# One decoder layer on one core: the down projection in seven products of block pairs, with sums of halves made ahead

## The chip, the cores and the metric

The kernel runs on 1 core of one Trainium2 chip. Its time is the device time of one execution in microseconds; the time of a kernel is the median of its runs. The profile is of one execution, taken by the hardware profiler. Of the engines, TensorE (PE) multiplies matrices, VectorE (DVE), ScalarE (ACT) and GpSimd (POOL) work on tiles elementwise, and SyncE (SP) issues most transfers. Each engine runs its instructions in the order in which they are written, and SP's transfers form one queue.

## The reference

A decoder layer on x of 1024 rows (T) by 1024 columns (D): two attention mixers, a SwiGLU feed-forward of width 2816 (F), layer norm after each, and scale, shift and gate from a conditioning vector c. The change is in the feed-forward:

```python
def swiglu(u, w_gate_up, w_down):
    h = jnp.einsum('btd,df->btf', u, w_gate_up)
    hg, hu = jnp.split(h, 2, axis=-1)
    return jnp.einsum('btf,fd->btd', jax.nn.silu(hg) * hu, w_down)
...
    x = layer_norm(DEEPNORM_ALPHA * x + (1.0 + gate_m) * y, ln1_g[l], ln1_b[l])
    u = x * (1.0 + scale_f) + shift_f
    y = swiglu(u, w_gate_up[l], w_down[l])
    x = layer_norm(DEEPNORM_ALPHA * x + (1.0 + gate_f) * y, ln2_g[l], ln2_b[l])
```

All of it is float32. `gate_f` is one of six vectors of 1024 that come from c through w_ada.

## The kernel before

**Numbers.** A float32 operand is split into a high part, which ScalarE rounds to fp32r, and a low part, which VectorE makes as the difference. A product of two operands is then three matmuls (high by high, high by low, low by high), each of 128x128 by 128x512 (`mac`, L191 to L193). `split` (L169, L170) does this for a whole operand; class `Pairs` does it for the weights of gate and up (L144, L145), and class `Weights` for others (L78, L79).

**Gate and up.** The loop over p (22 values, `NF`) makes 128 columns of F at a time for gate and up, all 1024 rows. Gate and up by the two halves of D, times the two halves of D by the two halves of the rows, would be eight products of halves; the kernel makes seven, some of them of sums (`product`, L1033, with its matmul L1041). A pass is one p: seven products, i = 0 to 6, of 12 matmuls each (4 blocks of D by three). POOL makes the sums of the weights for the next pass (`gu.add`, L126 to L132), SP loads those of the pass after that (`gu.load`, L112, two loads of 128x1024, 512 KB each), and a product's weights are split three products ahead (`g_prepare(n + 3)`). The bank of a product is copied by ScalarE (L1551, L1557) or added by VectorE (L1561) to what becomes the gate `g[0]` and `g[1]`, one for each half of the rows. At i = 6 VectorE multiplies gate and up (L1567, L1568), and SP stores both halves of h to scratch `h_d` (L1570).

Beside the loop run generators that move one step at a time: `last_ada` makes the gate vector `gates[5]` in steps at i = 3 and 6, with its weights in the tiles a_raw and a_lo and its sum in another; `ada_steps` does the like for other vectors earlier in the kernel, with L1009 as its matmul. Both split an accumulated sum and sum it over the partitions with a matmul by ones.

**Down projection.** h times w_down: 8 blocks of 128 rows by 2 halves of 512 columns by 22 blocks of F, three matmuls each, 1056. The weights are multiplied by `gates[5]` on POOL (L62) before they are split, so that the product can be added as it is. F is taken in groups:

```python
groups = [2, 3, 4, 3, 3, 3, 4]
```

For a group, every block of rows and every half of the columns gets a bank (`pd`), the matmuls of the group's F, and one VectorE addition into the row of z (L1627, 112 of them). While a group runs, the h of the next is loaded (`h_load`) and split (`h_prepare`), and the weights by `ws.step`. In the last group the statistics of each finished half row are taken (`half_stats`, L1272), and each row is normalized: `norm_shared` for the first seven (ScalarE, then its `finish` on VectorE and POOL, L1303 and L1304, and the store), and the shorter `norm_quick` (L1287 to L1292) for the last.

**Order.** It is written by hand (`tc.manual_schedule`): each engine runs its instructions in the program's order. A tile of a pool with n buffers waits until the n-th tile before it in that pool and tag is done with.

Of the kernel before, what the change touches and what calls it, by code (L numbers as in the profile page):

```python
# [149 lines left out]
def decoder_layer(ctx: ExitStack, tc: tile.TileContext, I, out, dbg=None):  # L150
# [83 lines left out]
    groups = [2, 3, 4, 3, 3, 3, 4]  # L234
    down_pool = lambda f: "low" if sum(f >= e for e in np.cumsum(groups)) % 2 else "bigu"
    for f in range(NF):
        for c in range(2):
            ws.add(I["w_down"][f * P:(f + 1) * P, c * 512:(c + 1) * 512], 1,
                   lambda c=c: gates[5][:, c * 512:(c + 1) * 512],
                   pair_dest(wd_t, f, lambda f: down_pool(f), "wd"))  # L240
# [744 lines left out]
    def ada_steps():  # L985
        for m in (2, 3, 4):
# [12 lines left out]
            if m == 2:  # L999
# [4 lines left out]
                yield  # L1004
                for t in range(2):
                    s = slice(t * TH, (t + 1) * TH)
                    ps = ps_2.tile([P, TH], F32, name="p2")
                    for x in range(2):
                        nc.tensor.matmul(ps, ones_r, hl[x][:, s], start=x == 0, stop=x == 1)  # L1009
# [591 lines left out]
    f0, ends, nxt = 0, [], 3  # L1601
    for gi, n in enumerate(groups):
        fs = range(f0, f0 + n)
        f0 += n
        last = gi == len(groups) - 1
        todo = [] if last else list(range(f0, f0 + groups[gi + 1]))
        prepare_at = {0: (), 3: (1, 3, 5), 4: (1, 2, 4, 6)}[len(todo)]
        for f in todo[:2]:
            if f not in h_raw:
                h_load(f)  # L1610
        for tb in range(NB):
            c = slice(tb * P, (tb + 1) * P)
            if tb in prepare_at:
                f = todo.pop(0)
                h_prepare(f)
                ws.step()
                ws.step()
                if len(todo) > 1:
                    h_load(todo[1])
            for eh in range(2):  # L1620
                es = slice(eh * 512, (eh + 1) * 512)
                pd = ps_f.tile([P, TH], F32, name="pf")
                for i, f in enumerate(fs):
                    wd, h = wd_t[f][0], hs[f]
                    mac(pd, (h[:, 0, c], h[:, 1, c]), (wd[:, 0, es], wd[:, 1, es]), i == 0, i == n - 1)
                z = zrow(tb)[:, es]
# [87 lines left out]
```

## Time and profile before

| | us |
|---|---|
| median of 3 runs (lowest, highest) | 1805.76 (1805.56, 1806.23) |
| the profiled execution | 1804.71 |
| its span (first to last instruction) | 1802.9 |
| gate and up, p = 0 to 21 | 1152.67 to 1555.60 |
| down projection, first to last matmul | 1555.60 to 1794.97 |
| after the last matmul | 7.93 |

The span is what the profile shows from the first instruction to the last; the profiled execution took 1.8 us more, and 1.05 us less than the median of the runs. The times of all views are counted from the start of the span. Each engine has a row of busy time; the row PEclk is the clock that TensorE was granted in 40 equal slices, where 9 is 90% or more. The chain of waits follows the work that ended last back from the end.

### The profile page before, as it was taken

Reading aid. Unit: us, or ns where it says so; the run is one execution under the profiler, and the core shown is the slowest. Engines: PE = TensorE matmul, PEld = TensorE weight load, DVE = VectorE, ACT = ScalarE, POOL = GpSimd, SP = SyncE. Lnnn points to the kernel's source line nnn. Section 1 sums busy time; section 2 is a strip of 40 time slices with the busy share of each in tenths; the row PEclk is TensorE's granted clock in tenths of the full one; section 3 lists DMA queues with packets and bytes.
Section 4 is the critical chain, followed back from the end, with each engine's and each line's share of the span. In section 5 each row is a group of like instructions: output and inputs, shape, how many; then the busy total and the mean of one; then the engine's idle time right before and its main releaser. Section 6 shows DMA issues by size and latency. Waiting matters only on the chain.

```text
span 1802.9 us, 24555 instructions
## 1 busy us (share of the span) xinstructions
PE 1786.3 (99%) x8906; PEld 1469.5 (82%) x8906; DVE 1147.7 (64%) x2051; ACT 810.3 (45%) x1720; POOL 619.2 (34%) x401
## 2 busy tenths in 40 slices
PE   9999999999999999999999999999999999999998
PEld 7888888888888888888788888888888888888886
DVE  7655566566656776558657865766675444764567
ACT  6544544444445677764442224734333333321122
POOL 0232233233233332125205644156663333531223
PEclk9999999999999999999999999999999999999999
DMA  9222333333332332266576333153332222442222
GB/s 363 88 71 81 97 85 92 100 87 106 90 83 83 91 94 72 79 237 234 181 231 238 144 108 109 36 166 110 110 101 86 82 82 88 163 139 72 97 73 93
DMA packets 93081, 213.83 MB, mean 119 GB/s; under 512 B 15072, under 2 KB 24864, under 8 KB 92960
## 3 DMA queue, kind: packets, MB, share of 16 engines
q1 hardware_dynamic: 92352, 210.61, 35.6%
q8 instruction: 70, 1.15, 0.3%
q0 software_dynamic: 464, 1.58, 0.2%
q14 instruction: 51, 0.42, 0.1%
q10 hardware_dynamic: 144, 0.07, 0.0%
HBM read 163.62 MB, written 34.96 MB: 110 GB/s over the span
## 4 chain that ended last, share of the span: by engine, by line
PE 94%; DVE 3%; ACT 2%; issue 1%; POOL 0%; DMA 0%; DVEq 0%; ACTq 0%
PE pf L1041 23%; PE pj L191 9%; PE pj L193 9%; PE pj L192 8%; PE p L1041 6%; PE pf L191 5%; PE pf L193 5%; PE pf L192 5%; PE s L628 4%; PE p L191 3%; PE p L193 3%; PE p L192 3%; PE po L689 3%; PE pt L666 3%; DVE qs L570 1%; ACT probs L644 1%
## 5 line engine op out<-in xcount | busy, mean ns | idle before, releaser
L191 PE MATMUL pj<-u,w_hi 128*128 128x512 f32 x736 | 302.5, 411 | 0.0
L193 PE MATMUL pj<-u,w_lo 128*128 128x512 f32 x736 | 288.6, 392 | 0.0
L192 PE MATMUL pj<-u,w_hi 128*128 128x512 f32 x736 | 288.1, 391 | 0.0
L555 POOL TENSOR_TENSOR rb<-rb,sin_t 128x512 f32<-128x512 f32 x64 | 85.6, 1338 | 518.1 <-DVE rb L553 464.5
L145 DVE TENSOR_TENSOR w_lo<-r,w_hi 128x512 fp32r<-128x512 f32 x128 | 140.2, 1099 | 118.7 <-ACT w_hi L144 118.3
L79 DVE TENSOR_TENSOR w_lo<-w_raw,w_hi 128x512 fp32r<-128x512 f32 x132 | 124.8, 949 | 81.3 <-ACT w_hi L78 80.8
L191 PEld LDWEIGHTS pj<-u,w_hi 128*128 128x128 f32 x736 | 138.5, 188 | 31.7 <-issue 5.8
L193 PEld LDWEIGHTS pj<-u,w_lo 128*128 128x128 f32 x736 | 138.2, 188 | 30.7
L644 ACT ACTIVATE probs<-probs,st 128x128 f32<-128x128 f32 (+1 forms) x320 | 145.6, 461 | 31.0 <-DVE st L633 30.6
L192 PEld LDWEIGHTS pj<-u,w_hi 128*128 128x128 f32 x736 | 138.8, 189 | 22.4
L62 POOL TENSOR_TENSOR w_raw<-w_raw,gate 128x512 f32<-128x512 f32 x60 | 86.3, 1453 | 148.4 <-DMA w_raw<-in_w_down 122.7
L191 PE MATMUL pf<-wd,h 128*128 128x512 f32 x352 | 136.9, 389 | 0.0
L192 PE MATMUL pf<-wd,h 128*128 128x512 f32 x352 | 136.9, 389 | 0.0
L193 PE MATMUL pf<-wd,h 128*128 128x512 f32 x352 | 136.9, 389 | 0.0
L1627 DVE SCALAR_TENSOR_TENSOR zt<-zt,pf 128x512 f32<-128x512 f32 x112 | 75.2, 684 | 79.4 <-PE pf L193 79.4
L78 ACT ACTIVATE w_hi<-w_raw 128x512 fp32r<-128x512 f32 x132 | 81.7, 622 | 92.7 <-PE p L192 53.2
L556 POOL TENSOR_TENSOR r<-ra,rb 128x512 f32<-128x512 f32 x63 | 115.8, 1838 | 4.9
L668 ACT ACTIVATE ptsb<-pt 128x512 f32<-128x512 f32 (+1 forms) x128 | 63.6, 549 | 101.2 <-PE pt L666 100.9
L569 ACT ACTIVATE qs<-r 64x1024 fp32r<-64x1024 f32 x38 | 40.2, 1058 | 100.4 <-POOL r L556 99.9
L570 DVE TENSOR_TENSOR qs<-r,qs 64x1024 fp32r<-64x1024 f32 x38 | 46.4, 1220 | 57.2 <-ACT qs L569 56.5
L628 PE MATMUL s<-kh,qs 128*128 128x256 f32 (+1 forms) x320 | 79.8, 283 | 1.8 <-DVE st L633 1.7
L126 POOL TENSOR_TENSOR s<-r 128x512 f32<-128x512 f32 x27 | 36.1, 1336 | 128.1 <-DVE w_lo L145 96.4
(393 smaller groups left out, 4438.2 us busy)
## 6 DMA issues: line engine op xcount, KB each, us to landing
w_raw<-in_w_in SPq DMA_DIRECT2D x100, 256.0 KB
r<-in_w_gate_up SPq DMA_DIRECT2D x44, 512.0 KB
a_raw<-in_w_ada SPq DMA_DIRECT2D x32, 512.0 KB
w_raw<-in_w_down SPq DMA_DIRECT2D x44, 256.0 KB
h_raw<-h_d SPq DMA_DIRECT2D x22, 512.0 KB
h_d<-g SPq DMA_DIRECT2D x39, 256.0 KB
wa<-in_w_ada_m SPq DMA_DIRECT2D x16, 512.0 KB
gt<-ga_d SPq DMA_DIRECT2D x16, 512.0 KB
```

The lines of the kernel that those rows point to most:

```text
L62: self.nc.gpsimd.tensor_tensor(self.raws[i], self.raws[i], scale(), op=OP.mult)
L78: self.nc.scalar.activation(hi, raw, AF.Copy)
L79: self.nc.vector.tensor_tensor(lo, raw, hi, op=OP.subtract)
L145: self.nc.vector.tensor_tensor(lo, src, hi, op=OP.subtract)
L191: nc.tensor.matmul(ps, w[0], m[0], start=first, stop=False)
L192: nc.tensor.matmul(ps, w[0], m[1], start=False, stop=False)
L193: nc.tensor.matmul(ps, w[1], m[0], start=False, stop=last)
L555: eng.tensor_tensor(b, b, sin_t[:, s], op=OP.mult)
L556: eng.tensor_tensor(residue_half(res, r, t), by_residue(a, r), by_residue(b, r), op=OP.add)
L628: nc.tensor.matmul(pss[h][:, i, lo:], box["q"][h][:, b * P:(b + 1) * P], ks[h][:, (b - 1 + lo) * P:(b + 1) * P], start=i == 0 and n == 0, ...
L644: nc.scalar.activation(pr, pr, AF.Exp, scale=-1.0, bias=st[:, 0, h, b:b + 1], accum_out=st[:, 1, h, b:b + 1])
L1041: nc.tensor.matmul(ps, w[:, c], m[:, k], start=first and k == 0 and n == 0, stop=k == 3 and n == 2, skip_group_check=True)
```

## The change

The down projection is made like gate and up: F is taken in 11 pairs of blocks (2j, 2j + 1), the rows and the columns in halves, and the eight products of halves of a pair become seven, of which five use sums of blocks. The products run one after the other over all 11 pairs, i = 0 to 6, each with 12 matmuls for a pair (4 blocks of rows by three): 7 x 11 x 12 = 924. An operand (`dn_op`) holds a half of 512 rows of h, or a sum of such halves, beside 512 columns of w_down, or a sum; the gate is multiplied in on VectorE when a bank is added to z (`dn_add`).

The sums of w_down and of h are made while gate and up run. A set is one pair j of weights ("w") or of h ("h"): two loads of 512 KB, four VectorE operations in two groups, two stores of 512 KB to scratch (`wt2_d`, `hs_d`). Two lanes make them, a step for each i: one from p = 8 in the tiles a_raw and a_lo, the other from p = 11 in the tile gb; the 22nd set runs in the down projection (`last_set`). `last_ada` therefore takes its steps at four places of a pass in place of two. The last pass (p = 21) loads and splits the first 12 of the 77 operands (`dn_prepare(2 * i, ...)`, two a product); from then on the operands are split 12 ahead and loaded 4 ahead of that. The last product (i = 6) runs one block of rows at a time, so that rows are finished in turn; the first four rows are normalized in it, and the last four behind it.

`ada_steps` gets one more yield behind its split.

```diff
@@ -1002,6 +997,7 @@
                 hl = [mix.tile([P, T], F32R, name="a_hl", tag="a_raw", bufs=2) for _ in range(2)]
                 split(*hl, acc)
                 yield
+                yield
                 for t in range(2):
...
@@ -1509,15 +1505,72 @@
-    def h_load(f):
...
-    def h_prepare(f):
...
+    NP = NF // 2
+    sets = [(kind, j) for kind in "wh" for j in range(NP)]
+
+    def sum_set(kind, j, x, y):
+        for i, tile in enumerate((x, y)):
+            f = 2 * j + i
+            nc.sync.dma_start(tile, I["w_down"][f * P:(f + 1) * P, :] if kind == "w" else h_d[f])
+        yield
+        yield
+        x0, x1, y0, y1 = x[:, H0], x[:, H1], y[:, H0], y[:, H1]
+        tt = nc.vector.tensor_tensor
+        if kind == "w":
+            tt(x0, x1, x0, op=OP.subtract)
+            tt(x1, y1, x1, op=OP.subtract)
+            yield
+            tt(y1, y1, x0, op=OP.subtract)
+            tt(y0, y0, y1, op=OP.subtract)
+        else:
...
+        yield
+        yield
+        for i, tile in enumerate((x, y)):
+            nc.sync.dma_start((wt2_d if kind == "w" else hs_d)[j, 2 * i:2 * i + 2].rearrange("s p c -> p s c"),
+                              tile.rearrange("p (s c) -> p s c", s=2))
+        yield
+
+    lanes = [iter(()), iter(())]
+
+    def sums_ahead(p, i):
+        for lane, first in enumerate((8, 11)):
+            if i == 1 and p >= first and sets and (sets[0][0] == "w" or 2 * sets[0][1] + 1 < p):
...
+                lanes[lane] = sum_set(*sets.pop(0), *tiles)
+            next(lanes[lane], None)
...
+    def dn_load(upto):
+        while len(dn_raw) < min(upto, DN):
+            u = len(dn_raw)
+            i, j = divmod(u, NP)
+            raw = gx.tile([P, 2, TH], F32, name="dn", tag="r1" if u % 2 else "r2", bufs=2)
...
+    def dn_prepare(upto, ahead):
+        while len(dn_op) < min(upto, DN):
+            u = len(dn_op)
+            dn_load(u + 1)
+            dn_op[u] = pools["bigu" if u % 14 < 8 else "low"].tile([P, 2, 2, TH], F32R, name="dn", tag="big")
+            split(dn_op[u][:, 0], dn_op[u][:, 1], dn_raw[u])
+            dn_load(u + 1 + ahead)
@@ -1575,65 +1628,73 @@
             else:
                 if i == 0:
-                    h_load(0)
-                    h_load(1)
-                    for j in range(3):
-                        ws.scale(len(ws.done) + j)
-                if i in (2, 4):
-                    h_prepare(i // 2 - 1)
-                    h_load(i // 2 + 1)
-                for _ in range({2: 2, 3: 1, 5: 1}.get(i, 0)):
-                    ws.step()
+                    dn_load(2)
+                dn_prepare(2 * i, 2 if i < 4 else 4)
+            sums_ahead(p, i)
...
-            if p > 1 and i in (3, 6):
+            if p > 1 and i in (1, 3, 4, 6):
                 next(ada, None)
...
-    for gi, n in enumerate(groups):
...
+    def dn_add(tb, eh, ps, first):
+        es = slice(eh * 512, (eh + 1) * 512)
+        z = zrow(tb)[:, es]
+        tmp = ev.tile([P, TH], F32, name="g", bufs=4)
+        nc.vector.tensor_tensor(tmp, ps, gates[5][:, es], op=OP.mult)
+        nc.vector.scalar_tensor_tensor(z, z, ALPHA if first else 1.0, tmp, op0=OP.mult, op1=OP.add)
...
+    for i in range(6):
...
+        for j in range(NP):
+            u = i * NP + j
+            dn_prepare(u + 12, 4)
+            for t in range(4):
+                dn_mac(ps[t], u, t, i in (0, 1, 3) and j == 0, j == NP - 1)
+            next(last_set, None)
...
+        for t in range(4):
+            dn_add(tb0 + t, eh, ps[t], first)
+            if not first:
+                half_stats(tb0 + t, eh)
...
+    for t in range(4):
+        for j in range(NP):
+            dn_mac(bank_a[t], 6 * NP + j, t, False, j == NP - 1)
+            if j == 5:
+                for _ in range(2 if t < 2 else 0):
+                    ends.append(norm_shared(todo.pop(0), gb2, out))
+                while len(ends) > 1:
+                    ends.pop(0)()
+        dn_add(4 + t, 0, bank_a[t], True)
+        half_stats(4 + t, 0)
+        while ends:
+            ends.pop(0)()
+        if t == 3:
+            norm_quick(7, gb2, out)
+        else:
+            ends.append(norm_shared(4 + t, gb2, out))
```

**Where the order moves.** The rows below are each engine's instructions in their order: line, operation, result<-operands, shape of the tile, and in brackets the engines and DMA queues' semaphores that are waited for.

First SP, in a pass in the middle of gate and up. Before, between the two stores of h of one pass (L1570) and those of the next stand the two loads of the weights of gate and up (L112; r_ are their tiles):

```order
L112 DMA r_12842<-in_w_gate_up 128x1024 [waits DMAHW1_49,DVE_49]
L112 DMA r_12843<-in_w_gate_up 128x1024 [waits DMAHW2_49,DVE_49]
L1570 DMA h_d<-g 128x512 [waits DMAHW3_49,DVE_49]
L1570 DMA h_d<-g 128x512 [waits DMAHW4_49,DVE_49]
L112 DMA r_12984<-in_w_gate_up 128x1024 [waits DMAHW5_49,DVE_49]
L112 DMA r_12985<-in_w_gate_up 128x1024 [waits DMAHW6_49,DVE_49]
```

Now, in a pass in which both lanes work on sets of h (a_raw and a_lo are the first lane's tiles, gb the second's):

```order
L1623 DMA h_d<-g 128x512 [waits DVE_49] x2
L1534 DMA hs_d<-a_raw 128x2x512 [waits DMAHW5_49]
L1534 DMA hs_d<-a_lo 128x2x512 [waits DMAHW6_49]
L1534 DMA hs_d<-gb 128x2x512 [waits DMAHW7_49]
L1534 DMA hs_d<-gb 128x2x512 [waits DMAHW0_49]
L1514 DMA a_raw<-h_d 128x1024 [waits DMAHW5_49,DMAHW1_49]
L1514 DMA a_lo<-h_d 128x1024 [waits DMAHW6_49,DMAHW2_49]
L1514 DMA gb<-h_d 128x1024 [waits DMAHW7_49,DMAHW3_49,DMAHW0_49]
L1514 DMA gb<-h_d 128x1024 [waits DMAHW4_49]
L112 DMA r_13444<-in_w_gate_up 128x1024 [waits DVE_49]
L112 DMA r_13445<-in_w_gate_up 128x1024 [waits DVE_49]
```

The stores of the sums of the sets before stand right behind the stores of h; the loads of the next sets wait for those stores; and the loads of gate and up's weights stand behind all of them.

Second VectorE, in the same kind of pass. Before, from the middle of a pass to its end (w_lo are the low parts of the splits, g the gates, L1567 and L1568 the two halves of h):

```order
L145 TENSOR_TENSOR w_lo<-r_12843,w_hi 128x512 [waits DMAHW2_49,DVE_49,Activation_49]
L145 TENSOR_TENSOR w_lo<-r_12842,w_hi 128x512 [waits DVE_49,Activation_49]
L145 TENSOR_TENSOR w_lo<-r_12843,w_hi 128x512 [waits DVE_49,PE_49,Activation_49]
L145 TENSOR_TENSOR w_lo<-r_12984,w_hi 128x512 [waits DVE_49,DMAHW5_49,PE_49,Activation_49]
L1561 TENSOR_TENSOR g<-g,pf 128x512 [waits DMAHW4_49,PE_49]
L145 TENSOR_TENSOR w_lo<-r_12984,w_hi 128x512 [waits DVE_49,Activation_49]
L1567 TENSOR_TENSOR g<-g,pf 128x512 [waits PE_49]
L1568 TENSOR_TENSOR g<-g,c_13123 128x512 [waits Pool_49]
```

Now, the same stretch of a pass with two sets of h:

```order
L145 TENSOR_TENSOR w_lo<-r_12639,w_hi 128x512 [waits DVE_49,Activation_49]
L1526 TENSOR_TENSOR a_lo<-a_raw,a_lo 128x512 [waits DMAHW6_49,DMAHW5_49,DMAHW2_49]
L1527 TENSOR_TENSOR a_raw<-a_raw 128x512 [waits DMAHW1_49,DVE_49]
L1526 TENSOR_TENSOR gb<-gb 128x512 [waits DMAHW4_49,DMAHW7_49,DMAHW3_49,DMAHW0_49]
L1527 TENSOR_TENSOR gb<-gb 128x512 [waits DVE_49]
L145 TENSOR_TENSOR w_lo<-r_12640,w_hi 128x512 [waits PE_49,Activation_49]
L1529 TENSOR_TENSOR a_raw<-a_lo,a_raw 128x512
L1530 TENSOR_TENSOR a_lo<-a_lo,a_raw 128x512 [waits DVE_49]
L1529 TENSOR_TENSOR gb<-gb 128x512
L1530 TENSOR_TENSOR gb<-gb 128x512 [waits DVE_49]
L145 TENSOR_TENSOR w_lo<-r_12800,w_hi 128x512 [waits PE_49,Activation_49]
L1614 TENSOR_TENSOR g<-g,pf 128x512 [waits PE_49]
```

Two groups of four operations stand between three splits of weights, and the first of them wait for the loads of the sets.

Third ScalarE, in the last pass (p = 21). Before, from the second product's gate to the copy of the fourth (h_raw is a block of h that is loaded, w_raw a block of w_down that POOL has scaled):

```order
L1563 ACTIVATE g<-g 128x512 [waits DVE_49]
L144 ACTIVATE w_hi<-r_13411 128x512 [waits DMAHW2_49,Activation_49,Pool_49]
L1551 ACTIVATE g<-pf 128x512 [waits DMAHW4_49,PE_49]
L169 ACTIVATE h<-h_raw 128x1024 [waits DMAHW2_49]
L78 ACTIVATE wd<-w_raw 128x512 [waits Pool_49] x2
L144 ACTIVATE w_hi<-r_13410 128x512 [waits Pool_49]
L1557 ACTIVATE c_13692<-pf 128x512 [waits PE_49]
```

Now, the same stretch (dn are the operands of the down projection, loaded and split):

```order
L1616 ACTIVATE g<-g 128x512 [waits DVE_49]
L169 ACTIVATE dn<-dn 128x1024 [waits DMAHW4_49,DMAHW3_49]
L169 ACTIVATE dn<-dn 128x1024 [waits DMAHW6_49,DMAHW5_49]
L144 ACTIVATE w_hi<-r_13601 128x512 [waits DMAHW0_49,Activation_49,Pool_49]
L1604 ACTIVATE g<-pf 128x512 [waits DMAHW2_49,PE_49]
L169 ACTIVATE dn<-dn 128x1024 [waits DMAHW7_49,DMAHW0_49]
L169 ACTIVATE dn<-dn 128x1024 [waits DMAHW2_49,DMAHW1_49]
L144 ACTIVATE w_hi<-r_13600 128x512 [waits Pool_49]
L1610 ACTIVATE c_13899<-pf 128x512 [waits PE_49]
```

Two operands now stand ahead of each split of the weights that the pass still needs.

More of the change, by code (lines that the diff above doesn't have):

```diff
@@ L217, in decoder_layer @@
         add_chunk(branch_w[b][dc], 1, 4)
-    late, wd_t, pools = {}, {}, {"bigu": bigu}
+    late, pools = {}, {"bigu": bigu}
     def pair_dest(store, key, pool, name):
@@ L233, in decoder_layer @@
     branches_end = len(ws.jobs)
[L234 to L240, printed above, removed]
     ph1 = ExitStack()
@@ L1269, in half_stats @@
     def half_stats(tb, eh):
-        if eh == 0:
+        if tb not in bst:
             bst[tb] = misc.tile([P, 2, 6], F32, name="bst", bufs=3)
@@ L1511, in decoder_layer @@
     ada = last_ada()
-    hs, h_raw = {}, {}
-    def h_load(f):
-        h_raw[f] = gx.tile([P, T], F32, name="h_raw", tag="r1" if f % 2 else "r2", bufs=2)
-        nc.sync.dma_start(h_raw[f], h_d[f])
-    def h_prepare(f):
-        hs[f] = pools[down_pool(f)].tile([P, 2, T], F32R, name="h", tag="big")
-        split(hs[f][:, 0], hs[f][:, 1], h_raw.pop(f))
+    NP = NF // 2
[15 more added lines that the diff above has]
+        else:
+            tt(y1, x1, y1, op=OP.add)
+            tt(x1, x0, x1, op=OP.subtract)
+            yield
+            tt(x0, y1, x0, op=OP.subtract)
+            tt(y0, y0, x0, op=OP.subtract)
+        yield
[3 more added lines that the diff above has]
+                              tile.rearrange("p (s c) -> p s c", s=2))
+        yield
@@ L1598, in decoder_layer @@
     gb2 = norm_params(2)
-    f0, ends, nxt = 0, [], 3
-    for gi, n in enumerate(groups):
[L1603 to L1626, printed above, removed]
-                nc.vector.scalar_tensor_tensor(z, z, ALPHA if gi == 0 else 1.0, pd, op0=OP.mult, op1=OP.add)
-                if last:
-                    half_stats(tb, eh)
-                    if eh == 0 and tb:
-                        ends.pop(0)()
-            if last:
-                if tb == NB - 1:
-                    norm_quick(tb, gb2, out)
-                else:
-                    ends.append(norm_shared(tb, gb2, out))
@@ new lines, in dn_add, with dn_mac @@
+    def dn_add(tb, eh, ps, first):
[4 more added lines that the diff above has]
+        nc.vector.scalar_tensor_tensor(z, z, ALPHA if first else 1.0, tmp, op0=OP.mult, op1=OP.add)
+    def dn_mac(ps, u, t, first, last):
+        op, c = dn_op[u], slice(t * P, (t + 1) * P)
+        for n, (x, y) in enumerate(((0, 0), (0, 1), (1, 0))):
+            nc.tensor.matmul(ps, op[:, x, 0, c], op[:, y, 1], start=first and n == 0, stop=last and n == 2,
+                             skip_group_check=True)
@@ new lines, in decoder_layer @@
+    st8 = gx.tile([P, TH], F32, name="s3", bufs=1)
+    for tb in range(NB):
+        bst[tb] = st8[:, tb * 12:(tb + 1) * 12].rearrange("p (a b) -> p a b", a=2)
+    bank_a = [ps_f.tile([P, TH], F32, name="pf") for _ in range(4)]
+    bank, ends = None, []
+    last_set = sum_set(*sets.pop(0), *[ev.tile([P, T], F32, name=n, tag=n, bufs=1) for n in ("a_raw", "a_lo")])
+    for i in range(6):
+        if i in (1, 3):
+            bank = [(ps_f, ps_x)[t // 2].tile([P, TH], F32, name=("pf", "px")[t // 2]) for t in range(4)]
+        ps = bank if i % 2 else bank_a
+        for j in range(NP):
[4 more added lines that the diff above has]
+            next(last_set, None)
+        tb0, eh, first = {0: (0, 0, True), 1: (0, 0, False), 2: (0, 1, True), 3: (4, 1, True), 4: (4, 1, False),
+                          5: (0, 1, False)}[i]
+        for t in range(4):
+            dn_add(tb0 + t, eh, ps[t], first)
+            if not first:
+                half_stats(tb0 + t, eh)
@@ new lines, in decoder_layer @@
+    dn_prepare(DN, 4)
+    todo = list(range(4))
+    for t in range(4):
[12 more added lines that the diff above has]
+            norm_quick(7, gb2, out)
+        else:
+            ends.append(norm_shared(4 + t, gb2, out))
```

18 lines of the change are left out of this document (15 added, 3 removed).

## The prediction

> **What bounds the kernel now.** I read the page first: its span, the engines' shares, the clock row and the chain of work that ended last.
>
> ```profile
> span 1802.9 us, 24555 instructions
> ...
> PE 1786.3 (99%) x8906; PEld 1469.5 (82%) x8906; DVE 1147.7 (64%) x2051; ACT 810.3 (45%) x1720; POOL 619.2 (34%) x401
> ...
> PEclk9999999999999999999999999999999999999999
> ...
> PE 94%; DVE 3%; ACT 2%; issue 1%; POOL 0%; DMA 0%; DVEq 0%; ACTq 0%
> ```
>
> TensorE is busy from end to end at a full granted clock, and 94% of the chain is its own. So a matmul taken out of a stage without gaps is worth its pitch, and everything else is worth what it makes TensorE wait. Next the busy time by stretches: the down projection, one pass of gate and up (one p, seven products), and the tail.
>
> ```profile
> core 0: us, PE busy (x) PEld busy (x) DVE busy (x) ACT busy (x) POOL busy (x), PEclk, DMA share, GB/s
> 1555.60:1794.97 239.37, 239.35 (x1056) 197.85 (x1055) 152.01 (x224) 53.80 (x75) 68.65 (x47) 1.00 0.29 101
> 1403.11:1422.15 19.04, 19.04 (x85) 15.77 (x84) 9.21 (x12) 7.30 (x13) 6.83 (x5) 1.00 0.23 83
> 1794.97:1802.90 7.93, 0.00 (x0) 0.00 (x0) 4.71 (x8) 0.20 (x1) 2.27 (x1) 0.76 0.34 132
> ```
>
> Both stages are full. The down projection's 1056 matmuls take 239.35 us, 0.2267 us each. A product of gate and up has 12 of them, 2.72 us, and a pass lasts 19.04 us, in which VectorE has 9.2 us of work and the DMA engines are busy for 23%. That is the room the new sums go into.
>
> **What is removed.** Eleven pairs of blocks x seven products x 12 matmuls are 924 instead of 1056. 132 x 0.2267 = **-29.9 us**. The 44 scalings on POOL (L62) and the 44 half-width splits go too; they stood beside TensorE and are worth nothing. The added yield in the second ada step moves the matmuls of gate 2 one product later, behind VectorE's split, and takes away this idle time (in brackets), **-1.4 us**:
>
> ```profile
> 872.51 0.96 PE L1009 MATMUL p<-a_hl,ones 128*128 128x512 f32 x3 [1.44 <-DVE a_hl L170]
> ```
>
> **The down projection itself** must keep up. Groups by shape:
>
> ```profile
> L1627 DVE SCALAR_TENSOR_TENSOR zt<-zt,pf 128x512 f32<-128x512 f32 x112 | 75.2, 684 | 79.4 <-PE pf L193 79.4
> L170 DVE TENSOR_TENSOR h<-h_raw,h 128x1024 fp32r<-128x1024 f32 x22 | 27.6, 1256 | 3.7 <-ACT h L169 3.7
> L169 ACT ACTIVATE h<-h_raw 128x1024 fp32r<-128x1024 f32 x22 | 23.2, 1054 | 67.7 <-DMA h_raw<-h_d 38.1 <-DVE zt L1627 29.6
> L1272 DVE BATCH_NORM_STATS2 bst<-zt 128x6 f32<-128x512 f32 x27 | 18.7, 693 | 0.8
> ```
>
> An operand pair costs ScalarE 1.05 and VectorE 1.26 us, and TensorE uses it for 2.72. With 28 additions of two instructions (56 x 0.68 = 38) and 16 statistics (11) VectorE has 77 x 1.26 + 49 = 146 us in 209. The runs of 8 to 12 instructions at the end of a product (5 to 8 us) are covered by operands 12 ahead (33 us). The loads are 77 x 512 KB in 209 us, 193 GB/s, about half of what the queue has carried (below). I cost all this at nothing. If that cover went, VectorE's surplus over 2.72 us would be paid per operand.
>
> **The sums in gate and up** decide the forecast. For p = 8 to 20 one set (two loads, four VectorE instructions, two stores of 512 KB) runs in each pass, and for p = 11 to 18 a second one. What a pass looks like now, from the timeline:
>
> ```profile
> 1403.31 0.69 DVE L1567 TENSOR_TENSOR g<-g,pf 128x512 f32<-128x512 f32 x1
> 1403.92 0.68 DVE L1568 TENSOR_TENSOR g<-g,c 128x512 f32<-128x512 f32 x1
> 1404.03 0.93 SPq L1570 DMA_DIRECT2D h_d<-g  x2
> ...
> 1410.63 1.29 POOL L128 TENSOR_TENSOR s<-s,r 128x512 f32<-128x512 f32 x1
> 1410.66 1.80 DVE L145 TENSOR_TENSOR w_lo<-r,w_hi 128x512 fp32r<-128x512 f32 x1 [1.22 <-ACT w_hi L144]
> 1412.62 0.69 DVE L145 TENSOR_TENSOR w_lo<-r,w_hi 128x512 fp32r<-128x512 f32 x1 [0.16 <-ACT w_hi L144]
> 1415.34 0.69 DVE L145 TENSOR_TENSOR w_lo<-r,w_hi 128x512 fp32r<-128x512 f32 x1 [2.03 <-ACT w_hi L144]
> ```
>
> VectorE runs instructions of this size 0.61 us apart, and 0.7 to 1.1 longer where POOL holds it up (1.80 beside 1.29). The new instructions of a pass stand between the splits for its sixth product (1412.62) and its seventh (1415.34, needed by TensorE 16.8 us into the pass). They wait for loads; the loads wait until the stores of the set before have left the same buffers; and those stores stand in SP's queue behind the two stores of h, which wait for the last instruction of the pass before (L1568). That closes a **ring**. Its transfers:
>
> ```profile
> 786.00:804.00 18.00, 17.94 (x81) 14.89 (x81) 11.72 (x15) 11.41 (x16) 6.45 (x7) 1.00 1.04 389
> 1405.00:1406.00 1.00, 1.00 (x6) 0.84 (x5) 0.21 (x1) 0.00 (x0) 0.00 (x0) 1.00 1.04 389
> 1406.00:1407.00 1.00, 1.00 (x6) 0.80 (x6) 0.00 (x0) 0.97 (x2) 0.00 (x0) 1.00 0.24 88
> 1592.00:1593.00 1.00, 1.00 (x6) 0.84 (x5) 1.00 (x2) 0.11 (x1) 1.00 (x1) 1.00 0.70 205
> ```
>
> A full queue carried 389 GB/s for 18 us; the stores of h went at 389 and were through at 1406.24, 1.64 us behind L1568's end. How long a load takes to be seen after its data I take from a pair issued alone:
>
> ```profile
> 1628.81 0.93 SPq L55 DMA_DIRECT2D w_raw<-in_w_down  x2
> ...
> 1631.63 2.54 POOL L62 TENSOR_TENSOR w_raw<-w_raw,gate 128x512 f32<-128x512 f32 x2 [8.12 <-DMA w_raw<-in_w_down]
> ```
>
> 2.82 us, less 0.46 for the issue and 0.67 for 256 KB, leaves 1.7; half of it, 0.8, is put behind the data. So one turn of the ring in a pass with two sets: 1.64 for h, 8 x 512 KB = 4.19 MB at 389 GB/s = 10.8, landing 0.8, then on VectorE 11 instructions (sets of weights) or 12 (sets of h) to the last product of h, 7.0, and 0.7 for one meeting with POOL: 20.9 us against 19.04. VectorE and SP are then 1.9 us late in each of the passes 12 to 18, and TensorE waits for the low half of a split. Added up: the ring starts 1.5 us into pass 12; six turns (125.4), 13.2 of transfers and 5.6 on VectorE later the low half for pass 19 is ready, at 145.7; TensorE wanted it at 7 x 19.04 + 0.45 = 133.7. **+12.0 us.** With one set a pass the transfers are half as long, and nothing waits. Bounds: 0 if the turn stays under 19.04; at the poorest rate for a share (205 at 0.70, 293 GB/s) 4.19 MB take 14.3, and the cost is 12.0 + 7 x 3.5 = 36.
>
> [...]
>
> **The last pass** now prepares 12 operands. ScalarE's queue has two of them (1.05 each, with VectorE's 1.26 behind) ahead of each split that TensorE needs two products later, and until the last weights are split only two buffers turn: the next pair is loaded when VectorE is done with the last. From pair to pair: 1.05 + 1.26 + 2.82 for a load alone + 1.1 for its second half = 6.2 us, where a product takes 2.72. The first pair follows the stores of the set of pass 20: 1.5 + 1.64 + 2.7 + 1.35 + 0.8 = 8.0 us into the pass; the third pair then starts at 20.4, its second half 1.5 later; with its split, the weights' split of 0.6 and VectorE's 1.26 + 0.69 the seventh product has its low half at 25 and ends at 27 instead of 19.04. The trace has no such queue; bounds 2 (loads come early) and 9. I take **+7.5**.
>
> **The tail.** The chain's last rows, and POOL beside them:
>
> ```profile
> 1794.99 0.70 DVE zt L1627
> 1795.72 0.71 DVE bst L1272
> ...
> 1796.84 1.48 DVE zt L1287
> ```
>
> ```profile
> 1793.61 1.21 DVE L1303 TENSOR_TENSOR zt<-zt,gb 128x1024 f32<-128x1024 f32 x1
> 1794.89 2.34 POOL L1304 TENSOR_TENSOR zt<-zt,gb 128x1024 f32<-128x1024 f32 x1 [3.04 <-DVE zt L1303]
> ```
>
> Each result now needs a multiplication by the gate before it is added (+0.7), and block 6's L1303 and L1304 move behind the last matmul: +1.2 on VectorE, and L1287 then waits for some 1.9 us of POOL's 2.34 instead of 0.4 (+1.5). **+3.4.**
>
> **The sum.** -29.9 - 1.4 + 12.0 + 7.5 + 3.4 = -8.4 us. The profiled execution took 1804.71 us (span 1802.9), 1.05 under the median of 1805.76; the forecast is 1805.76 - 8.4, **1797 us**.
>
> **Rivals.** *The sums fit*: the ring stays under 19.04 us, because loads land sooner or stores and loads overlap, and the last pass loses 2 to 7.5. For it: VectorE has half of each pass free, and 1.9 us is a small excess. Against it: every member of the ring is in one order. -29.9 - 1.4 + 3.4 + 2 to 7.5 gives 1780 to 1785.
>
> *The ring costs more than the products save*, and the kernel is slower. The point is where 7 x (turn - 19.04) - 1.3 = 29.9 + 1.4 - 7.5 - 3.4 = 20.4: a turn of 22.1 us, 4.19 MB at 350 GB/s. At 293 it is 24.4, and the time 1805.76 - 8.4 + 24.5 = 1822; at 330 it is 1810. For it: short windows with scratch transfers reach only 205 at 0.70. Against it: 389 GB/s held in a long queue, which this is.
>
> *The change doesn't do what it says* (matmuls not fewer) is ruled out by the order: 924 in place of 1056. *The down projection falls behind its operands*, and VectorE's or the DMA queue's pace replaces 2.72 us: each 0.1 us is 7.7 us, 1805 at 2.82. Against it: 146 us in 209, and half the queue's rate.
>
> **Chances.** Forecast (1788 to 1805) 0.47, sums fit 0.25, slower through the ring 0.21, down projection behind 0.07. The range takes in the forecast's, the first rival and the lower half of the second: 1780 to 1814. A difference under 0.2% (3.6 us) can't be told from none here. Faster takes the first rival, most of the forecast and a little of the last: 0.63. Within 0.2%: 0.14. Slower: 0.23.
>
> **What would show it.** TensorE's idle time in passes 12 to 18 put down to VectorE's split (L145), and VectorE's before it to loads of the sums; a pass of some 21 us there and 19.04 before; the passes from 19 at 19.04, the last one some 7 us longer; the down projection at 924 matmuls in 209 to 211 us without gaps; a tail of some 11 us. Wrong: passes 12 to 18 at 19.04 (first rival), or at over 22 us (second), or gaps inside the down projection.

## The result, and the profile after

The changed kernel is **slower: 1854.9 us** median of 6 runs (1852.39 to 1858.02) against 1805.8 (6 runs, 1805.56 to 1806.85), a ratio of 1.0273 (95% interval 1.026 to 1.0286). The prediction of 1797 (1780 to 1814) was wrong. The profiled execution has a span of 1852.7 us, 49.8 more than before.

The same rows of the page, after the change: span, engines, granted clock, chain of waits.

```profile
span 1852.7 us, 24551 instructions
...
PE 1783.3 (96%) x8774; PEld 1458.4 (79%) x8774; DVE 1214.1 (66%) x2094; ACT 843.3 (46%) x1731; POOL 562.9 (30%) x357
...
PEclk9999999999999999999999999999999999899998
...
PE 73%; DVE 11%; DMA 7%; issue 3%; ACT 3%; SPq 2%; POOL 1%; DVEq 0%; ACTq 0%; POOLq 0%
```

132 matmuls fewer, but TensorE's share of the chain falls from 94% to 73%; VectorE and transfers have taken its place. The waits of TensorE from gate and up to the start of the down projection, in groups (who waited for whom, us in total, times, longest):

```profile
PE pf L1037 <- DVE w_lo L145: 32.3, 15, 4.0
PE pf L1037 <- ACT g L1604: 4.6, 1, 4.6
PE pf L1037 <- ACT c L1610: 4.3, 2, 2.8
```

And the busy time by stretches: pass 3, a pass with one set (10), two with two sets (13 and 16), the last pass, the down projection, the tail (columns as before).

```profile
1199.67:1220.36 20.69, 16.73 (x62) 13.02 (x61) 15.20 (x11) 5.22 (x10) 13.66 (x7) 0.85 0.57 177
...
1341.51:1362.25 20.74, 19.42 (x86) 15.61 (x84) 14.60 (x16) 7.31 (x14) 12.81 (x7) 1.00 0.50 178
1407.18:1430.57 23.39, 20.94 (x86) 16.83 (x85) 15.55 (x21) 7.30 (x13) 6.81 (x5) 0.93 0.68 247
1477.99:1502.58 24.59, 20.99 (x86) 16.85 (x85) 14.50 (x20) 7.30 (x13) 7.10 (x5) 0.93 0.65 235
1590.97:1623.90 32.93, 23.14 (x75) 16.60 (x74) 17.19 (x18) 13.21 (x17) 2.60 (x2) 0.79 0.63 203
1623.90:1833.50 209.60, 209.60 (x925) 173.24 (x923) 144.68 (x169) 82.03 (x82) 11.32 (x5) 1.00 0.57 195
1833.50:1852.70 19.20, 0.03 (x1) 0.00 (x0) 14.98 (x20) 3.01 (x5) 6.62 (x3) 0.55 0.31 122
```

The down projection is what the change said: 209.6 us without a gap. Everything else got longer. By stages (a pass ends where VectorE starts on its first product of h, L1567 or now L1620), in us:

| stage | before | after | difference | predicted |
|---|---|---|---|---|
| up to the end of pass 2 | 1196.53 | 1199.67 | +3.1 | -1.4 |
| passes 3 to 8 | 111.16 | 119.21 | +8.1 | 0 |
| passes 9 to 11 | 57.54 | 65.07 | +7.5 | 0 |
| passes 12 to 20 | 171.36 | 207.02 | +35.7 | +12.0 |
| pass 21 up to the down projection | 19.01 | 32.93 | +13.9 | +7.5 |
| down projection, first to last matmul | 239.37 | 209.6 | -29.8 | -29.9 |
| after the last matmul | 7.93 | 19.2 | +11.3 | +3.4 |
| span | 1802.9 | 1852.7 | +49.8 | -8.4 |

### The profile page after: what moved, and what is told of

The parts are those of the page before. It is cut to its first block, busy times and chain, and to the rows that moved or that the text cites. A ratio compares the mean times of both kernels' runs of the same rounds, so it can differ in the third digit from the quotient of the medians.

```text
span 1852.7 us, 24551 instructions
## 1 busy us (share of the span) xinstructions
PE 1783.3 (96%) x8774; PEld 1458.4 (79%) x8774; DVE 1214.1 (66%) x2094; ACT 843.3 (46%) x1731; POOL 562.9 (30%) x357
## 3 DMA queue, kind: packets, MB, share of 16 engines
q0 software_dynamic: 464, 1.58, 0.2%
## 4 chain that ended last, share of the span: by engine, by line
PE 73%; DVE 11%; DMA 7%; issue 3%; ACT 3%; SPq 2%; POOL 1%; DVEq 0%; ACTq 0%; POOLq 0%
PE pf L1037 9%; PE pj L191 8%; PE pj L193 8%; PE pj L192 8%; PE pf L1655 7%; PE p L1037 6%; PE s L623 4%; PE p L191 3%; PE p L193 3%; PE p L192 3%; PE po L684 3%; PE pt L661 2%; PE px L1655 2%; DVE w_lo L145 2%; DMA a_lo<-h_d 1%
## 5 line engine op out<-in xcount | busy, mean ns | idle before, releaser
L145 DVE TENSOR_TENSOR w_lo<-r,w_hi 128x512 fp32r<-128x512 f32 x128 | 131.2, 1030 | 67.6 <-ACT w_hi L144 67.2
L1655 PE MATMUL pf<-dn 128*128 128x512 f32 x726 | 170.1, 389 | 0.0
L1655 PEld LDWEIGHTS pf<-dn 128*128 128x128 f32 x726 | 136.4, 188 | 28.4
L169 ACT ACTIVATE dn<-dn 128x1024 fp32r<-128x1024 f32 x77 | 81.7, 1061 | 113.8 <-DMA dn<-in_w_down 40.8
L170 DVE TENSOR_TENSOR dn<-dn 128x1024 fp32r<-128x1024 f32 x77 | 92.5, 1222 | 53.8 <-ACT dn L169 52.7
L1616 ACT ACTIVATE g<-g 128x512 f32<-128x512 f32 x39 | 24.7, 632 | 166.4 <-DVE g L1614 166.4
```

The costliest lines, as they stand in the source:

```text
L145: self.nc.vector.tensor_tensor(lo, src, hi, op=OP.subtract)
L170: nc.vector.tensor_tensor(lo, src, hi, op=OP.subtract)
L1655: nc.tensor.matmul(ps, op[:, x, 0, c], op[:, y, 1], start=first and n == 0, stop=last and n == 2, skip_group_check=True)
```

## The experiments

**The ring and its stores.** VectorE's timeline over one turn of pass 13, from the last product of h (L1621) to the next:

```profile
1407.78 0.69 DVE L1621 TENSOR_TENSOR g<-g,c 128x512 f32<-128x512 f32 x1
...
1418.85 0.69 DVE L1520 TENSOR_TENSOR a_raw<-a_raw 128x512 f32<-128x512 f32 x1 [3.10 <-DMA a_raw<-in_w_down]
1420.16 1.71 DVE L1521 TENSOR_TENSOR a_raw<-a_lo,a_raw 128x512 f32<-128x512 f32 x1 [0.61 <-DMA a_lo<-in_w_down]
1421.79 1.76 DVE L1520 TENSOR_TENSOR gb<-gb 128x512 f32<-128x512 f32 x1
1423.59 0.69 DVE L1521 TENSOR_TENSOR gb<-gb 128x512 f32<-128x512 f32 x1
1424.20 0.69 DVE L145 TENSOR_TENSOR w_lo<-r,w_hi 128x512 fp32r<-128x512 f32 x1
...
1428.06 0.68 DVE L1614 TENSOR_TENSOR g<-g,pf 128x512 f32<-128x512 f32 x1
1429.96 0.69 DVE L145 TENSOR_TENSOR w_lo<-r,w_hi 128x512 fp32r<-128x512 f32 x1 [1.22 <-ACT w_hi L144]
1430.57 0.68 DVE L1620 TENSOR_TENSOR g<-g,pf 128x512 f32<-128x512 f32 x1
1431.16 0.68 DVE L1621 TENSOR_TENSOR g<-g,c 128x512 f32<-128x512 f32 x1
```

The turn is 23.4 us. By its semaphore the last load of the second lane landed at 1423.38, 14.9 us behind the end of L1621 (1408.47); L1521 on gb starts right behind it (the 1.71 and 1.76 before it lie beside POOL's additions, L1618 of 1.29 us from 1420.03 and L130 of 1.73 from 1421.28), and from the landing to the end of the next L1621 (1431.84) are 8.5 us. In passes 12 and 16 the rows show VectorE idle for that lane's loads, until 15.0 and 15.6 us behind the end of L1621 (1385.23 and 1479.27):

```profile
1400.20 0.69 DVE L1521 TENSOR_TENSOR gb<-gb 128x512 f32<-128x512 f32 x1 [0.34 <-DMA gb<-in_w_down]
1494.88 0.69 DVE L1526 TENSOR_TENSOR gb<-gb 128x512 f32<-128x512 f32 x1 [1.86 <-DMA gb<-h_d]
```

If the ring is closed by the stores that the next loads wait for, issuing the stores before those of h opens it:

```diff
             tt(y0, y0, x0, op=OP.subtract)
         yield
-        yield
         for i, tile in enumerate((x, y)):
```

> The changed kernel with one yield taken out of a set, so that its stores are issued at i = 5 and no longer stand behind the stores of h. Theory (the ring is closed by the stores that the next loads wait for): the loads start 3 to 5 us earlier in the pass, the passes 12 to 18 fall from 23.2-24.6 to 19.0-20, -30 us, about 1825. Rival (the rate of the transfers or VectorE's own 11 instructions set the pass): less than 8 us.

1815.14 us (1813.37 to 1817.67), 39.8 less from one line. Passes 9 and 10 fall to 19.04, 12 to 18 to between 19.1 and 21.6. SP's part of the timeline shows the stores (L1533) 3 to 6 us ahead of those of h (L1622), and the loads (L1514) right behind h; the last load now lands 8.6 to 11.2 us behind the last product of h in these passes, in place of 13.8 to 15.4:

```profile
1452.73 0.38 SPq L1533 DMA_DIRECT2D hs_d<-a_raw  x1
1453.45 0.38 SPq L1533 DMA_DIRECT2D hs_d<-a_lo  x1
1454.05 2.40 SPq L1533 DMA_DIRECT2D hs_d<-gb  x2
1458.49 0.93 SPq L1622 DMA_DIRECT2D h_d<-g  x2
1459.52 0.47 SPq L1514 DMA_DIRECT2D a_raw<-h_d  x1
```

**The clock in the ring.** In the changed kernel the clock falls behind each wait of the passes 12 to 18. One microsecond a row, around the wait of the turn above (the matmul restarts at 1424.94):

```profile
1423.00:1424.00 1.00, 0.00 (x0) 0.00 (x0) 0.97 (x2) 0.00 (x0) 0.01 (x1) 1.00 0.09 37
1424.00:1425.00 1.00, 0.06 (x1) 0.06 (x1) 1.00 (x3) 0.00 (x0) 0.00 (x0) 1.00 0.01 4
1425.00:1426.00 1.00, 1.00 (x5) 0.81 (x6) 0.96 (x2) 0.00 (x0) 0.00 (x0) 0.97 0.12 37
1426.00:1427.00 1.00, 1.00 (x4) 0.81 (x3) 0.96 (x3) 0.00 (x0) 0.00 (x0) 0.50 0.99 315
...
1429.00:1430.00 1.00, 1.00 (x5) 0.83 (x4) 0.04 (x1) 1.00 (x3) 0.00 (x0) 0.83 0.00 0
```

The granted clock goes to 0.50 a microsecond after the matmuls have restarted (1425.94), and stays there for 3.41 us; behind the seven waits of these passes it falls 0.5 to 1.5 us after the restart. To see what that is worth, filler matmuls keep TensorE busy in the wait:

```diff
+                if fill and k == 0 and n == 2:
+                    px = ps_x.tile([P, TH], F32, name="px")
+                    for f in range(fill):
+                        nc.tensor.matmul(px, hi[:, c], b[0][:, k], start=f == 0, stop=f == fill - 1)
...
+                product(..., fill=9 if i == 6 and 12 <= p <= 18 else 0)
```

> The changed kernel with 9 matmuls (9 x 0.227 = 2.0 us) of no use, into a bank of their own, ahead of the matmul that waits for the low half in each of the passes 12 to 18. Theory: TensorE's wait falls from 2.45 to 3.6 us to 0.4 to 1.6 us, the granted clock stays at 1.00, and each of the seven passes gets about 1.7 us shorter although work is added: -12 us, about 1843. Rival (the clock costs nothing, the ring alone sets the pass): no change, or up to 14 us longer.

The clock did stay at 1.00 in these passes (the mean clock of the profiled execution was 0.989 instead of 0.982; seven stretches of 3.41 us at 0.50 lower it by 0.0065), and the theory still fell: 1851.48 us (1850.57 to 1856.21), 3.4 less, a difference that the spread of the runs does not make sure, and passes 12 to 18 took 162.8 us instead of 166.4. VectorE's end of a turn, with the filler:

```profile
1452.00 0.68 DVE L1618 TENSOR_TENSOR g<-g,pf 128x512 f32<-128x512 f32 x1
1453.90 0.69 DVE L145 TENSOR_TENSOR w_lo<-r,w_hi 128x512 fp32r<-128x512 f32 x1 [1.22 <-ACT w_hi L144]
1454.51 0.68 DVE L1624 TENSOR_TENSOR g<-g,pf 128x512 f32<-128x512 f32 x1
```

VectorE goes from the gate's addition (L1618) over a split that waits 1.22 us for ScalarE (whose queue has the gate's silu first) to the product of h, without a wait for TensorE. The ring runs over VectorE, and a slow TensorE is mostly hidden in it.

**What a wait costs by itself.** In the kernel before, a split for the seventh product is repeated, so that TensorE waits in an otherwise undisturbed pass of 19.04 us:

```diff
-        self.nc.vector.tensor_tensor(lo, src, hi, op=OP.subtract)
+        for _ in range(1 + (LADDER.get(p, 0) if i == 6 else 0)):
+            self.nc.vector.tensor_tensor(lo, src, hi, op=OP.subtract)
```

> The kernel before, with VectorE's split for the seventh product done 10 to 17 times over in the passes 10 to 19 (9, 10, 11, 12, 12, 13, 13, 14, 14 and 16 repeats, 0.61 us each), so that TensorE waits longer and longer for the same operand. It measures what an idle time costs beyond itself. Theory: up to about 2.0 us the clock stays at 1.00 and a pass grows by the wait plus 0.3; from 2.2 us on the clock is at 0.50 for some 3 us behind the wait, and the pass grows by 1.7 more. Rival (the wait costs only itself): each pass grows by its wait plus 0.3, and the clock row stays at 1.00.

The repeats took 0.73 us each and started from a longer wait than I had reckoned: 1905.8 us, all waits between 5.5 and 10.2 us, and no answer on which waits leave the clock at 1.00. It shows only that the clock fell while TensorE still stood: 2.3 us after it had stopped in the wait of 10.2 (from 1343.6 on), 3.2 in that of 5.5 (from 1376.8 on). So a second one:

> The same kernel as in the run with 9 to 16 repeats, whose waits of 5.5 to 10.2 us all brought the clock to 0.50, now with 4, 5, 5, 6, 6, 6, 7, 7, 8 and 9 repeats in the passes 10 to 19, so that the waits should be 0.8 to 4.5 us. Theory: waits up to 2.0 us leave the clock at 1.00 and add themselves and 0.3; waits from 2.2 us on add 1.7 to 2 more. Rival (the clock falls only behind waits of over 3.2 us, the time after which it fell within the long ones): the waits of 2.3 to 3.0 us add only themselves and 0.3.

1853.73 us. Waits (in brackets, in TensorE's timeline) and the passes around them:

```profile
1396.35 0.50 PE L1045 MATMUL pf<-t4h,w_lo 128*128 128x512 f32 x1 [1.58 <-DVE w_lo L149]
1441.23 0.50 PE L1045 MATMUL pf<-t4h,w_lo 128*128 128x512 f32 x1 [2.31 <-DVE w_lo L149]
1488.49 0.51 PE L1045 MATMUL pf<-t4h,w_lo 128*128 128x512 f32 x1 [3.04 <-DVE w_lo L149]
1537.23 0.63 PE L1045 MATMUL pf<-t4h,w_lo 128*128 128x512 f32 x1 [3.76 <-DVE w_lo L149]
```

```profile
1382.91:1403.83 20.92, 19.34 (x86) 15.68 (x85) 13.63 (x16) 7.30 (x13) 7.25 (x6) 1.00 0.22 75
1426.69:1449.88 23.19, 20.88 (x85) 16.78 (x85) 14.36 (x18) 7.29 (x13) 7.27 (x5) 0.93 0.20 69
1472.61:1496.74 24.13, 21.09 (x86) 16.95 (x85) 15.23 (x19) 7.29 (x13) 7.27 (x5) 0.93 0.18 66
1520.82:1545.93 25.11, 21.35 (x87) 17.16 (x86) 16.20 (x20) 7.29 (x13) 7.27 (x5) 0.93 0.18 63
```

A wait of 1.58 makes the pass 1.88 longer (itself and 0.30), at a clock of 1.00. Those of 2.31, 3.04 and 3.76 shown make it 4.15, 5.09 and 6.07 longer, with a mean clock of 0.93; the two other waits of 2.31, in passes of 22.86 and 22.73 us, 3.8 and 3.7. Over all of them that is 1.1 to 2.0 us more than themselves and 0.30. All three waits of 2.31 us had half the clock behind them: the mean of their passes is 0.93, 0.93 and 0.92.

Nor does the length alone decide. In the changed kernel's profile a matmul is shown with 0.39 us at a clock of 1.00 and with 0.63 at 0.50. A wait of 1.89 us with early stores (up to 1082.09) had matmuls of 0.63 behind it; one of 1.88 in the second of these runs (up to 1375.44) and one of 2.01 in the changed kernel (1376.32 to 1378.33) had the clock at 1.00 behind them; of the changed kernel's waits from 1080 on every one of 2.20 or more had half the clock behind it or already in it. The clock's own entries in the changed kernel's profile bear on this: ahead of the last matmul it has 11 low stretches, eight of 3.41 us and three of 6.83, and all begin on one grid of 3.41 us. TensorE's idle time was added up in each step of that grid, for this one execution. Behind the 11 steps at full clock with 1.92 us idle or more the next step was at 0.50; behind the others, some 500 with 1.83 or less, it never was. The wait of 2.01 had 1.83 of it in one step; one of 2.45 (1445.89 to 1448.34), shared 0.53 and 1.92, was followed by half the clock. So in this profile the idle time within one step tells the waits with half the clock behind them (1.92 and more) from those without (1.83 and less). In the kernel before no step has over 1.44 us idle ahead of the last matmul, and the clock stays at 1.00 up to there.

**The steps of last_ada.** Pass 3 lost 6.0 us, with the row that shows why: VectorE stands on a load of w_ada, and the splits behind it come late.

```profile
1210.33 2.08 DVE L1491 SCALAR_TENSOR_TENSOR gate<-a_raw,c_act,gate 128x1024 f32<-128x1024 f32 x1 [4.27 <-DMA a_raw<-in_w_ada]
1212.33 5.60 DVE L145 TENSOR_TENSOR w_lo<-r,w_hi 128x512 fp32r<-128x512 f32 x2
```

With steps at i = 1, 3, 4 and 6 the load of step 1 is used at step 3, and SP issued it at 1203.79, as soon as its tile was free; before, the same load was issued at 1200.11 for a use at i = 6, at 1214.0. The edit lets the loads take the two tiles by turns, each a step ahead, at the old places:

```diff
-            raw = ev.tile([P, T], F32, name="a_raw", bufs=1)
-            nc.sync.dma_start(raw, I["w_ada"][k * P:(k + 1) * P, 5 * D:])
-            yield
+            if k < KC:
+                n = "a_lo" if k % 2 else "a_raw"
+                raws[k] = ev.tile([P, T], F32, name=n, tag=n, bufs=1)
+                nc.sync.dma_start(raws[k], I["w_ada"][k * P:(k + 1) * P, 5 * D:])
...
-            if p > 1 and i in (1, 3, 4, 6):
+            if p > 1 and i in (3, 6):
```

> The changed kernel with the steps of last_ada back at i = 3 and 6, each load a whole step ahead of its use in two tiles by turns. Theory: the wait of 3.96 us in pass 3 and the halved clock behind it go, and those of 0.3 to 1 us in passes 4 to 7: -8 us, about 1847. Rival (the wait in pass 3 comes from POOL's gain instructions): no change.

1850.23 us (1849.08 to 1852.15), 4.7 less. Passes 3 to 7 are as before the change (14.66, then 19.30, 19.30, 19.31 and 19.23), and passes 3 to 8 take 111.84 us instead of 119.21. Up to pass 2 the profiled execution gains another 2.5 (below, on the yield), and the untouched passes behind take 5.5 more, first of all pass 9 (24.83 instead of 22.63). That is not shown to be the edit's doing: passes 9 to 11 took 65.1 us in the profiled execution of the changed kernel, and 68.6 to 69.5 in those of all four versions that leave the stores and these passes alone. What a single edit to this kernel is worth is known to some 4 us only.

**The yield in the ada step alone**, in the kernel before:

```diff
                 split(*hl, acc)
                 yield
+                yield
```

> The kernel before with the added yield in the ada step alone. Forecast of the prediction: the idle time of 1.44 us at 872.5 goes, -1.4 us. Theory now: the time is given back later, where the load of a row of x lands later, TensorE waits 2.2 us instead of 0.85 at 1082, and its clock is halved for some 3 us behind that: +3 us in all, about 1809.

Neither: 1805.82 us, ratio 0.9998 (0.999 to 1.0007). The idle time at 872.5 goes, and at 1082 TensorE waits 1.79 us instead of 0.85 for VectorE, whose addition stands on a load of x; the next matmul starts at 1082.07, before at 1082.04. In the profiled execution of the changed kernel this wait was 2.20, and the clock was 0.58 in the 4 us from 1084 on: the +3.1 of the first stage. It belongs to that execution more than to the change, since in the other ten versions with the yield pass 2 ended at 1196.6 to 1200.0.

**The last pass alone**, on the changed kernel:

```diff
-                dn_prepare(2 * i, 2 if i < 4 else 4)
+                dn_prepare({3: 2, 5: 4, 6: 6}.get(i, 0), 4)
...
-            dn_prepare(u + 12, 4)
+            dn_prepare(min(u + 12, 2 * u + 8), 4)
```

> The changed kernel with six operands prepared in the last pass instead of 12: two at i = 3, behind the last split of the weights, two at i = 5, two at i = 6; the rest follow two for one at the start of the down projection. Theory (ScalarE's copies of the banks and its splits stand behind operands that wait for loads): TensorE's waits for L1604, L1610 and L145 in the last pass go, the pass falls from 32.6 to 19-21 us, -12 us, about 1843. Rival (operands come at the pace of their loads wherever they stand): the waits move into the first product of the down projection, under 5 us gained.

1841.21 us (1839.43 to 1841.71), 13.7 less; of the waits in the last pass only one of 1.10 us is left. The rows of the changed kernel that it answers to, ScalarE's in the last pass:

```profile
1602.20 1.06 ACT L169 ACTIVATE dn<-dn 128x1024 fp32r<-128x1024 f32 x1 [0.26 <-DMA dn<-in_w_down]
1603.17 0.61 ACT L144 ACTIVATE w_hi<-r 128x512 fp32r<-128x512 f32 x1
...
1603.69 0.58 ACT L1604 ACTIVATE g<-pf 128x512 f32<-128x512 f32 x1
```

The copy of the third product's bank (L1604) stands behind two operands and a split, and TensorE waits 4.6 us for it, since the fifth product writes to that bank. That product's own weights (L144) were ready only 0.5 us sooner, so it is the operands ahead of both that cost.

**The tail alone**, on the changed kernel, with product 5 ahead of 4 and the first four normalizations beside 4:

```diff
+    ORDER = (0, 1, 2, 3, 5, 4, 6)
...
+            if i == 4 and j in (3, 5, 7, 9):
+                while ends:
+                    ends.pop(0)()
+                ends.append(norm_shared((j - 3) // 2, gb2, out))
```

> The changed kernel with the products of the down projection in the order 0, 1, 2, 3, 5, 4, 6, so that the first four rows are finished one product earlier and normalized beside product 4, and with the finish of a row in the middle of the next row. Theory (VectorE's queue of the last product holds four normalizations too many, and is 8 us late when TensorE ends): the tail falls from 19.2 us to 9-11, about 1846. Rival (VectorE's work in the last two products is too much in either order): the tail stays over 15 us, or TensorE waits inside product 4.

1861.59 us (1855.96 to 1864.36), 6.7 more. The tail did fall to about 9 us, but ahead of product 6 TensorE waited 11.06 us: it goes on in the banks of product 4, which VectorE must first have read, and VectorE was late with that by the operations now put into product 4. The work only moved.

**Together.** First the stores, last_ada and the second lane one product later:

```diff
+        for _ in range(2 + late):
+            yield
...
-                lanes[lane] = sum_set(*sets.pop(0), *tiles)
+                lanes[lane] = sum_set(*sets.pop(0), *tiles, lane)
...
             if i == 6:
+                sums_ahead(p, i)
                 nc.vector.tensor_tensor(g[0], g[0], x, op=OP.mult)
```

> The changed kernel with the stores at i = 5 and last_ada at i = 3 and 6 together, and with the second lane's operations one product later (its stores at i = 6, ahead of the stores of h). Theory: both gains add up (-40 and -8), and the passes 11 to 18, still 19.1 to 21.6 with early stores because the second lane's loads land late, fall to 19.0-19.7: about 1797 to 1800. Rival (eight transfers of 512 KB beside the weights and h are too much for a pass): those passes stay at 20 to 21, about 1807.

1797.14 us (1796.9 to 1797.87), ratio to before 0.9951 (0.9936 to 0.9966). Between the passes 3 and 20 TensorE has no wait of 0.3 us or more. Then all four edits:

> The four edits together: early stores with the second lane one product later, last_ada at i = 3 and 6 in two tiles, six operands in the last pass, and the order 0, 1, 2, 3, 5, 4, 6. Theory: the 29.4 us that the down projection saves remain, and 1 to 4 us of losses: about 1775 to 1780. Rival: one of the waits only moves on, and the time stays over 1790.

1790.69 us (1789.15 to 1793.74): over what the theory said, mostly by the wait of 11.2 us ahead of product 6. So without the new order of products:

> Early stores with the second lane one product later, last_ada at i = 3 and 6 in two tiles, and six operands in the last pass; the products of the down projection in the order of the changed kernel, as the other order made TensorE wait 11 us for the bank of product 4. Theory: the gap of 11.2 us goes, the tail is again 19 us instead of 9: about 1788. Rival: the tail of 19 us comes from the late start of the down projection's operands and is under 14 us here: about 1782.

**1787.06 us** (1785.71 to 1788.46), ratio 0.9896 (0.9882 to 0.9911): faster than both. Its stretches, a pass with two sets, the last pass, the down projection, the tail:

```profile
1403.00:1422.00 19.00, 19.00 (x85) 15.76 (x84) 15.38 (x20) 7.26 (x14) 7.06 (x5) 1.00 0.85 300
1536.48:1555.50 19.02, 19.02 (x85) 15.55 (x84) 10.10 (x12) 8.52 (x13) 2.80 (x2) 1.00 0.46 149
1555.50:1765.10 209.60, 209.54 (x925) 173.18 (x923) 151.85 (x174) 86.92 (x86) 11.40 (x5) 1.00 0.62 209
1765.10:1783.90 18.80, 0.00 (x0) 0.00 (x0) 14.98 (x20) 2.92 (x5) 6.53 (x3) 0.56 0.31 122
```

Pass 20 ends at 1536.48, before the change at 1536.59. The sums cost gate and up nothing there, with the same loads, stores and operations. What is left of the loss is the tail. VectorE's groups of the last product and the tail in the changed kernel:

```profile
L1299 DVE TENSOR_TENSOR zt<-zt,gb 128x1024 f32<-128x1024 f32 x7 | 9.9, 1425 | 0.0
L1650 DVE SCALAR_TENSOR_TENSOR zt<-zt,g 128x512 f32<-128x512 f32 x6 | 7.3, 1223 | 0.2
L1295 DVE SCALAR_TENSOR_TENSOR brs<-bmv,brs 128x1 f32<-128x1 f32 x7 | 5.6, 794 | 0.2
```

L1650 takes 0.69 us elsewhere, and L1295 0.16 in four of its seven instances: beside POOL's additions (L1300, 2.57 us on average) the one takes 2.40 and 2.17 and the other 1.60 to 1.72, and the means here are 1.22 and 0.79. Hence the last edit, these additions on VectorE, and the finish of two rows moved:

> The same, with the addition of the norm's offset on VectorE instead of POOL, and the finish of rows 5 and 6 in the middle of the next row. Theory (a VectorE operation that meets POOL's 2.4 us addition takes 1.4 to 2.6 us longer, seven times, where the same addition on VectorE takes 1.2): the tail falls from 19 to some 13 us, 5 us less than the kernel without it. Rival (VectorE has only more to do): no gain, or up to 8 us longer.

No gain that can be told: 1786.04 us (1785.16 to 1787.27) against 1787.06, ratio to before 0.9891 (0.9875 to 0.9908), tail 19.6. A meeting with POOL's addition had cost VectorE 1.4 to 2.0 us in the rows, not up to 2.6. L1653 (the former L1650) is back at 0.69 and L1295 at 0.16, but seven additions of 1.23 us have come into the same queue. How the last product's work on VectorE could be made less was not tried.

## Why the prediction was wrong

- **Removed products.** Right: -29.8, predicted -29.9, and no gap in the down projection.
- **The ring.** Right as a mechanism: the early stores took away 39.8 us. The step that failed is the size of the turn, "20.9 us against 19.04": over passes 12 to 18 it was 23.8 on average, and they lost 33.1 us instead of 12 to 13. Both of its terms were too small. The transfers, reckoned at 1.64 + 10.8 + 0.8 = 13.2, took 14.7 on average to the last load's landing (13.8 to 15.4). VectorE, reckoned at 7.0 + 0.7, took 9.1 from there. In pass 13 its 11 instructions took the 7.0, but between the gate's addition and the next split it stood 1.22 us for ScalarE, whose silu and high half come first; the sum had no such term. Why the transfers took longer was not tested; the second lane's loads were issued only at 1416.98, when its stores had landed, and the queue carried 221 GB/s in the microsecond from 1415 and 414 and 426 in those from 1418. The clock has some 3 to 4 of the 33 us, by the filler's run. The turn is past the point of 22.1 that the rival "the ring costs more than the products save" named, and the transfers, by whose rate that rival had it, are half of the reason.
- **"With one set a pass ... nothing waits."** Wrong: passes 9 and 10 lost 4.8 us, and pass 11, the first with a second set, 2.8. The loads stood behind the stores and h here as well, and VectorE waited for them ahead of a split. With early stores passes 9 and 10 cost nothing.
- **last_ada.** Not in the sum at all. The diff's new places of its steps shortened the time from load to use, and that cost 8.1 us in passes 3 to 8.
- **The yield.** -1.4 was given back 210 us later, at the next wait on loads, so that by itself it is worth nothing; the rest of the +3.1 is the clock behind a wait of 2.20 us in that execution.
- **The last pass.** +13.9 instead of +7.5. The path was the predicted one, from pair to pair (6.0 us from 1600.89 to 1606.96 and 1612.92, predicted 6.2) to the low half for the seventh product, but four terms were too small. The first pair started 9.9 us into the pass instead of 8.0; the second half of the third came 2.5 us behind the first instead of 1.5; VectorE's last split (L145) took 1.76 instead of 0.69; and the seventh product, at a clock of 0.50, took 4.4 us from its low half to its end instead of 2. The 8.9 us of waits for ScalarE's bank copies lie beside this path.
- **The tail.** +11.3 instead of +3.4. The working took VectorE to be in time at the last matmul. It was 7.5 us late: the last bank's multiplication by the gate (L1649) starts at 1840.99, the matmuls end at 1833.5. The meeting of the last norm with POOL, +1.5 in the prediction, was 1.7 (L1283 3.27 instead of 1.56, beside POOL's addition of 2.34).

## What to carry to other kernels

Work that is put beside a busy engine was not paid here by its share of busy time but by the order in which the queues pass it on: the passes 12 to 18 lost 33.1 us beside the sums in one order, and in another pass 20 ended at 1536.48, where it ended at 1536.59 without them. Follow each ring of store, load and operation through every queue, ScalarE's too, and count each step whose lead the diff shortens. Put a store where its data are ready, not behind the next thing that waits: one yield was worth 40 us here, and with it and edits of the same kind the changed kernel became faster than the one before. Idle times of TensorE of 2.31 us cost 3.7 to 4.2 here, one of 1.58 cost 1.88.

## What the runs showed of the hardware

- In the changed kernel's profile the granted clock changed only on a grid of 3.41 us up to the last matmul. When TensorE was idle for 1.92 us or more of a step at full clock, the next step was at 0.50, 11 times out of 11; with 1.83 us or less that never came, in some 500 steps. So the clock also fell after TensorE had started again, in the ring 0.5 to 1.5 us after.
- Keeping TensorE busy with filler matmuls held the clock at 1.00 in passes 12 to 18 (mean over the execution 0.989, without them 0.982), in 63 added matmuls (7 x 9), at no cost in time: 1851.48 us against 1854.9.
- The same wait at 1082 was 0.85 us before, and 1.53 to 2.20 in the versions with the added yield, though nothing near it was changed: the matmul behind it started no earlier than 1082.07 in any of them (before: 1082.04). Time won ahead of it was lost there.
